# Global attention in a hybrid encoder: the high and low parts of the probabilities side by side, as one moving operand of 512 columns

## The chip, the cores and the metric

The kernel runs on 1 core of one Trainium2 chip. The metric is the device time of one execution in microseconds (us). The kernel before takes 2157.99 us, the median of 3 runs (2155.97 to 2158.89).

## What is computed

One encoder layer is applied to a prompt of 1024 tokens and a sample of 256 tokens, each with 16 learned meta tokens in front of it, at a model width of 2048. A projection gives queries, keys, values and gates of two groups of 8 heads, of 128 numbers each. Group A attends globally, with 2 key and value heads shared by 4 query heads each; group B attends in a window around each token of a 64-wide grid, plus the meta tokens. The results are gated and go through an output projection. The change is in group A alone:

```python
def global_gqa(q, k, v):
    scale = HEAD_DIM ** -0.5
    def attend(qb):                      # a block of queries
        qg = qb.reshape(B, L, N_KV_A, G, HEAD_DIM)
        s = jnp.einsum('blkgd,bskd->bkgls', qg, k).astype(jnp.float32) * scale
        p = jax.nn.softmax(s, axis=-1).astype(v.dtype)
        o = jnp.einsum('bkgls,bskd->blkgd', p, v)
        return o.reshape(B, L, D_A)
    ...
ya = global_gqa(qa, ka, va) * jax.nn.silu(za)
```

Everything is float32.

## The kernel before

**Products in three parts.** TensorE (PE) takes most operands in a reduced form of float32 (`F32R`). To keep the precision, `split` (L65 to L67) makes two pieces of an operand: ScalarE (ACT) copies it into the reduced form, the high part, and VectorE (DVE) subtracts that from the full value, which leaves the low part. A product then takes three matmuls that add up in one PSUM tile: high by high, low by high, and high by low.

**Stages.** `chunk1` projects the sample's 256 tokens, 240 of the prompt's and the meta tokens, and attends for the sample. `chunk2` projects the prompt's other 784 tokens, attends globally for the whole prompt (head by head, each in 4 blocks of 256 queries), and then does the windowed heads. `outproj` is the output projection. In the profile shown here `chunk2`'s global blocks lie between about 700 and 1335 us.

**A global block** is one call of `attend`. For each pair of key tiles (128 keys each) three matmuls a tile (L377 to L379) put scores into `sp`; ACT copies them into a tile `S` (L381) and DVE keeps a running maximum (L385, L387). GpSimd (POOL) takes the maximum over partitions (`all_max`, L328); DVE subtracts it (L397), ACT takes the exponential (L398), and DVE and POOL make the sum (L401 to L407, L346). Then come the values: for each pair of key tiles `split` makes `ph` and `pl`, 512 columns each, from `S`, and for each key tile three matmuls of 256 columns add into `po`, with the transposed output of 128 rows by 256 queries:

```python
nc.tensor.matmul(po[:], vh, ph[:, i, :], start=j == 0, stop=False)    # L418
nc.tensor.matmul(po[:], vl, ph[:, i, :], start=False, stop=False)     # L419
nc.tensor.matmul(po[:], vh, pl[:, i, :], start=False, stop=False)     # L420
```

`vh` and `vl` are the two parts of the value tile, the stationary operand, which PE loads anew for each matmul. One matmul for the meta tokens ends the sum (L421). `put_y` turns the sum of probabilities into its reciprocal (L353 to L356), multiplies `po` by the gate (L362, DVE, or L359 in a windowed block), then by the reciprocal (L363), and stores the result (L364, on SyncE's queue SP).

The prompt has 8 heads with 4 blocks of 8 key tiles each, 256 key tiles in all. The sample has 8 heads with one block of 2 key tiles each, 16 in all.

**What sets the order.** Nothing here is ordered by hand: a scheduler with its own estimate of durations puts the instructions of each engine into one fixed order when the program is built. Every engine then works through its own list in that order. So between the matmuls of a block stand matmuls of the next head's projection (`pp`, L227 to L229), which fill the time in which a block waits for ACT, DVE and POOL. Buffers are limited: `po` has one buffer in PSUM (pool `op`), `ph` and `pl` have two each, `sp` two.

Of the kernel before, what the change touches and what calls it, by code (L numbers as in the profile page):

```python
# [12 lines left out]
F32 = mybir.dt.float32  # L13
F32R = mybir.dt.float32r
BF16 = mybir.dt.bfloat16
AF = mybir.ActivationFunctionType
ALU = mybir.AluOpType
# [4 lines left out]
P = 128  # L22
# [13 lines left out]
ALIGN = 128  # L36
# [4 lines left out]
QB = 256  # L41
# [18 lines left out]
class Kern:  # L60
# [288 lines left out]
    def put_y(self, po, tot, zs, ydst):  # L349

        nc = self.nc
        r = self.t.tile([P, QB], F32, tag="t", name="r")
        nc.scalar.activation(r[:], tot[:], AF.Ln)  # L353
        nc.scalar.activation(r[:], r[:], AF.Exp, scale=-1.0)
        nc.vector.tensor_tensor(out=tot[:], in0=tot[:], in1=r[:], op=ALU.mult)
        nc.vector.scalar_tensor_tensor(out=r[:], in0=tot[:], scalar=2.0, in1=r[:], op0=ALU.subtract, op1=ALU.mult)  # L356
        y = self.y.tile([P, QB], F32, tag="y", name="y")
        if len(zs.shape) == 3:
            nc.vector.tensor_tensor(out=y[:].rearrange("p (g r) -> p g r", g=4), in0=po[:].rearrange("p (g r) -> p g r", g=4),  # L359
                                    in1=zs, op=ALU.mult)  # L360
        else:
            nc.vector.tensor_tensor(out=y[:], in0=po[:], in1=zs, op=ALU.mult)  # L362
        nc.vector.scalar_tensor_tensor(out=y[:], in0=y[:], scalar=-1.0, in1=r[:], op0=ALU.mult, op1=ALU.mult)  # L363
        self.ystore = nc.sync.dma_start(ydst, y[:].rearrange("p (g r) -> p g r", g=ydst.shape[1])).ins  # L364

    def attend(self, q, zs, keys, meta, vals, vmeta, ydst):

        nc = self.nc
        nt = len(keys)
        qh, ql = q[:, 0, :], q[:, 1, :]  # L370
        S = []
        mx = None
        for p in range(nt // 2):
            ps = self.sp.tile([P, 2, QB], F32, tag="sp", name="sp")
            for i in range(2):
                kh, kl = keys[2 * p + i]
                nc.tensor.matmul(ps[:, i, :], kh, qh, start=True, stop=False)  # L377
                nc.tensor.matmul(ps[:, i, :], kh, ql, start=False, stop=False)  # L378
                nc.tensor.matmul(ps[:, i, :], kl, qh, start=False, stop=True)  # L379
            s = self.s.tile([P, 2, QB], F32, tag="S", name="S")  # L380
            nc.scalar.copy(s[:], ps[:])  # L381
            S.append(s)
            if p == 1:
                mx = self.mx.tile([P, 2, QB], F32, tag="mx", name="mx")
                nc.vector.tensor_tensor(out=mx[:], in0=S[0][:], in1=ps[:], op=ALU.max)  # L385
            elif p > 1:
                nc.vector.tensor_tensor(out=mx[:], in0=mx[:], in1=ps[:], op=ALU.max)  # L387
        pm = self.sp.tile([P, 2, QB], F32, tag="sp", name="sm_ps")
        sm = self.meta_scores(pm[:, 0, :], meta, qh, ql, 1.0)
        src = S[0] if mx is None else mx  # L390
        m1 = self.t.tile([P, QB], F32, tag="t", name="m1")
        nc.vector.tensor_tensor(out=m1[:], in0=src[:, 0, :], in1=src[:, 1, :], op=ALU.max)
        ma = self.all_max(m1, sm)
        mb = ma[:].unsqueeze(1).to_broadcast([P, 2, QB])
        for p in range(nt // 2):
            s = S[p][:]
            nc.vector.tensor_tensor(out=s, in0=s, in1=mb, op=ALU.subtract)  # L397
            nc.scalar.activation(s, s, AF.Exp, scale=SCALE)  # L398
            if p == 1:
                acc = self.mx.tile([P, 2, QB], F32, tag="mx", name="acc")  # L400
                nc.vector.tensor_tensor(out=acc[:], in0=S[0][:], in1=S[1][:], op=ALU.add)  # L401
            elif p > 1:
                nc.vector.tensor_tensor(out=acc[:], in0=acc[:], in1=s, op=ALU.add)
        pm3 = self.meta_probs(sm, ma, SCALE)
        src = S[0] if nt == 2 else acc
        a1 = self.t.tile([P, QB], F32, tag="t", name="a1")
        nc.vector.tensor_tensor(out=a1[:], in0=src[:, 0, :], in1=src[:, 1, :], op=ALU.add)  # L407
        tot = self.all_sum(a1, sm)
        yield
        po = self.op.tile([P, QB], F32, tag="po", name="po")  # L410
        for j in range(nt):
            p, i = divmod(j, 2)
            if i == 0:
                ph = self.ph.tile([P, 2, QB], F32R, tag="ph", name="ph", align_bytes=ALIGN)
                pl = self.ph.tile([P, 2, QB], F32R, tag="pl", name="pl", align_bytes=ALIGN)
                self.split(ph[:], pl[:], S[p][:])
            vh, vl = vals[j]
            nc.tensor.matmul(po[:], vh, ph[:, i, :], start=j == 0, stop=False)  # L418
            nc.tensor.matmul(po[:], vl, ph[:, i, :], start=False, stop=False)  # L419
            nc.tensor.matmul(po[:], vh, pl[:, i, :], start=False, stop=False)  # L420
        nc.tensor.matmul(po[:], vmeta, pm3[:], start=False, stop=True)  # L421
        self.put_y(po, tot, zs, ydst)

    def attend_sample(self, q, zs, k, km, vals, vmeta, tab, ydst):

        nc = self.nc
        ps = self.sp.tile([P, 2, QB], F32, tag="sp", name="sp")
        ps = ps[:].rearrange("p a b -> p (a b)")
        for i in range(2):
            nc.tensor.matmul(ps[:, HALF * i:HALF * i + HALF], k[:, P * i:P * i + P], q[:, 64 * i:64 * i + HALF], start=True, stop=True)  # L430
        pm = self.sp.tile([P, 2, QB], F32, tag="sp", name="sm_ps")
        hl = self.ph.tile([P, 2, QB], F32R, tag="ph", name="qhl", align_bytes=ALIGN)
        self.split(hl[:, 0, :], hl[:, 1, :], q)
        sm = self.meta_scores(pm[:, 0, :], km, hl[:, 0, :], hl[:, 1, :], SCALE)
        s = self.s.tile([P, 2, QB], F32, tag="S", name="S")
        s = s[:].rearrange("p a b -> p (a b)")
        w = 2 * HALF
        self.lasts = nc.vector.scalar_tensor_tensor(out=s[:, :w], in0=ps[:, :w], scalar=SCALE, in1=tab, op0=ALU.mult, op1=ALU.add).ins

        def ap(t, off, dims):  # L440
            return bass.AP(t.tensor, t.offset + off, [list(t.ap[0])] + dims)

        def gather(name, op):

            m = self.t.tile([P, QB], F32, tag="t", name=name)
            nc.vector.tensor_copy(ap(m[:], 0, [[192, 2], [1, 64]]), ap(s, 0, [[320, 2], [1, 64]]))
            nc.vector.tensor_tensor(out=m[:, 64:192], in0=s[:, 64:192], in1=s[:, 192:320], op=op)
            return m

        ma = self.all_max(gather("m1", ALU.max), sm)  # L450
        v = ap(s, 0, [[HALF, 2], [1, HALF]])
        nc.vector.tensor_tensor(out=v, in0=v, in1=ap(ma[:], 0, [[64, 2], [1, HALF]]), op=ALU.subtract)
        nc.scalar.activation(s[:, :w], s[:, :w], AF.Exp)
        pm3 = self.meta_probs(sm, ma, 1.0)
        tot = self.all_sum(gather("a1", ALU.add), sm)
        yield
        po = self.op.tile([P, QB], F32, tag="po", name="po")
        nc.tensor.matmul(po[:], vmeta, pm3[:], start=True, stop=False)
        for i in range(2):
            nc.tensor.matmul(po[:, 64 * i:64 * i + HALF], vals[:, i, :], s[:, HALF * i:HALF * i + HALF], start=False, stop=i == 1)  # L460
        self.put_y(po, tot, zs, ydst)

    def attend_strip(self, q, qf, zs, k, meta, vals, vmeta, tab, w, ydst):
# [3 lines left out]
        nc = self.nc  # L467
# [25 lines left out]
        def ap(t, off, dims):  # L493
            return bass.AP(t.tensor, t.offset + off, [list(t.ap[0])] + dims)
# [13 lines left out]
        v = ap(sb, 0, [[192, 2], [1, 192]])  # L508
        nc.vector.tensor_tensor(out=v, in0=v, in1=ap(ma[:], 0, [[64, 2], [1, 192]]), op=ALU.subtract)
        nc.scalar.activation(sb[:, :384], sb[:, :384], AF.Exp)  # L510
        pm3 = self.meta_probs(sm, ma, 1.0)
        tot = self.mx.tile([P, 2, QB], F32, tag="mx", name="tot")[:, 0, :]
        self.all_sum(gather("a1", ALU.add), sm, tot)
        yield
        po = self.op.tile([P, QB], F32, tag="po", name="po")
        nc.tensor.matmul(po[:], vmeta, pm3[:], start=True, stop=False)
        for t in (0, 3, 1, 2):
            a, e = groups[t]
            nc.tensor.matmul(po[:, 64 * a:64 * e], vals[:, t, :], part(sa, sb, t), start=False, stop=t == 2)  # L519
# [826 lines left out]
```

## Time and profile before

| What | us |
|---|---|
| Time, median of 3 runs | 2157.99 |
| Time of the profiled execution | 2156.31 |
| Its span, first to last instruction | 2154.5 |
| PE busy, 11745 matmuls | 2147.4 |
| PE loading weights (beside matmuls) | 1878.4 |
| DVE busy | 1666.1 |
| ACT busy | 1190.9 |
| POOL busy | 524.0 |

The span is the profiled execution's time but for 1.8 us. "Busy" adds up what an engine's instructions cover. The ends of matmuls are modelled, and consecutive matmuls overlap in the profile: one of 256 columns is shown as 0.28 us long while the next one starts 0.12 us after it. So a matmul's price is the distance between the starts of two in a row, not its length. PE's granted clock is 1.00 over the whole span. A wait is the idle time of an engine before an instruction; it is put down to the work that ended last before it.

### The profile page before, as it was taken

The page shows a single profiled execution, that of the slowest core. Times are in us where ns is not written, and L with a number is a line of the kernel's source. Part 1 is how long each engine was busy: PE and PEld are TensorE (multiplying, and loading weights), DVE is VectorE, ACT ScalarE, POOL GpSimd, SP SyncE. Part 2 cuts the span into 40 slices and gives each one's busy share as a digit, 9 for nine tenths or more (in the row PEclk, how much of TensorE's full clock was granted, in tenths as well). Part 3 has the DMA queues.
Part 4 walks back from the last instruction along what each step waited for, and adds up shares of the span by engine and source line. Part 5 has one row for each costly group of instructions (what it writes and reads, how often), then busy time and mean ns, then how long its engine had stood idle before and what let it go on. Part 6 is the DMA issues. An engine that isn't in the chain of part 4 may idle for free.

```text
span 2154.5 us, 34001 instructions
## 1 busy us (share of the span) xinstructions
PE 2147.4 (100%) x11745; PEld 1878.4 (87%) x11745; DVE 1666.1 (77%) x3013; ACT 1190.9 (55%) x2419; POOL 524.0 (24%) x250
## 2 busy tenths in 40 slices
PE   9999999999999999999999999999999999999999
PEld 7888888888888999998999999989999888888887
DVE  7698977788874899996799988777787786545763
ACT  7677644454665777776677775444444454232230
POOL 1142422222221223231133224333333311000000
PEclk9999999999999999999999999999999999999999
DMA  8666789988654333334233244554433364762663
GB/s 294 215 193 220 238 291 320 341 280 281 212 191 133 97 102 106 110 97 142 91 110 100 95 129 150 184 161 135 138 124 123 114 215 140 242 234 91 234 225 107
DMA packets 257420, 377.24 MB, mean 175 GB/s; under 512 B 43072, under 2 KB 108768, under 8 KB 257248
## 3 DMA queue, kind: packets, MB, share of 16 engines
q1 hardware_dynamic: 257248, 375.07, 53.7%
q8 instruction: 92, 1.51, 0.3%
q14 instruction: 80, 0.66, 0.1%
HBM read 281.01 MB, written 100.38 MB: 177 GB/s over the span
## 4 chain that ended last, share of the span: by engine, by line
PE 98%; DVE 1%; DMA 1%; SPq 0%; issue 0%; ACT 0%; DVEq 0%
PE pp L229 22%; PE pp L227 22%; PE pp L228 22%; PE pq L1072 6%; PE pq L1070 6%; PE pq L1071 6%; PE po L519 2%; PE sp L485 2%; PE sp L378 1%; PE sp L379 1%; PE po L420 1%; PE sp L377 1%; PE po L419 1%; PE po L418 1%; PE tp L540 0%; PE sm_ps L316 0%
## 5 line engine op out<-in xcount | busy, mean ns | idle before, releaser
L227 PE MATMUL pp<-x,wh 128*128 128x512 f32 (+1 forms) x1664 | 654.0, 394 | 0.6 <-ACT wh L66 0.3
L229 PE MATMUL pp<-x,wl 128*128 128x512 f32 (+1 forms) x1664 | 647.8, 390 | 0.2 <-DVE wl L67 0.2
L228 PE MATMUL pp<-x,wh 128*128 128x512 f32 (+1 forms) x1664 | 647.9, 390 | 0.0
L229 PEld LDWEIGHTS pp<-x,wl 128*128 128x128 f32 x1664 | 312.5, 188 | 61.4 <-DVE wl L67 0.8
L227 PEld LDWEIGHTS pp<-x,wh 128*128 128x128 f32 x1664 | 312.4, 188 | 55.6 <-ACT wh L66 2.0
L228 PEld LDWEIGHTS pp<-x,wh 128*128 128x128 f32 x1664 | 312.9, 188 | 51.9
L262 POOL PARTITION_ALL_REDUCE m<-ms x78 | 223.1, 2860 | 352.5 <-ACT ms L260 300.3
L67 DVE TENSOR_TENSOR wl<-wr,wh 128x512 fp32r<-128x512 f32 (+2 forms) x287 | 209.6, 732 | 107.2 <-ACT wh L66 80.4
L346 POOL PARTITION_ALL_REDUCE tot<-a x80 | 181.0, 2262 | 433.5 <-DVE a L343 419.8
L66 ACT CAST wh<-wr 128x512 fp32r<-128x512 f32 (+2 forms) x287 | 173.5, 611 | 162.5 <-PE pp L228 147.8
L228 PE MATMUL pp<-xb,wh 128*128 128x272 f32 x832 | 240.8, 289 | 0.0
L227 PE MATMUL pp<-xb,wh 128*128 128x272 f32 x832 | 239.6, 288 | 0.0
L229 PE MATMUL pp<-xb,wl 128*128 128x272 f32 x832 | 239.0, 287 | 0.0
L328 POOL PARTITION_ALL_REDUCE ma<-m x80 | 113.3, 1417 | 447.8 <-DVE m L326 436.3
L1072 PE MATMUL pq<-wm,yl 128*128 128x512 f32 x560 | 218.3, 390 | 0.6 <-DVE yl L67 0.6
L1070 PE MATMUL pq<-wm,yh 128*128 128x512 f32 x560 | 218.3, 390 | 0.0
L1071 PE MATMUL pq<-wm,yh 128*128 128x512 f32 x560 | 218.0, 389 | 0.0
L227 PEld LDWEIGHTS pp<-xb,wh 128*128 128x128 f32 x832 | 156.5, 188 | 7.5
L228 PEld LDWEIGHTS pp<-xb,wh 128*128 128x128 f32 x832 | 156.5, 188 | 7.4
L229 PEld LDWEIGHTS pp<-xb,wl 128*128 128x128 f32 x832 | 157.4, 189 | 0.1
L1072 PEld LDWEIGHTS pq<-wm,yl 128*128 128x128 f32 x560 | 105.1, 188 | 22.9 <-DVE yl L67 1.0
L1071 PEld LDWEIGHTS pq<-wm,yh 128*128 128x128 f32 x560 | 105.1, 188 | 21.6
(218 smaller groups left out, 3951.9 us busy)
## 6 DMA issues: line engine op xcount, KB each, us to landing
wr<-in_w_in SPq DMA_DIRECT2D x413, 256.0 KB, 3.5
wld<-wl SPq DMA_DIRECT2D x132, 256.0 KB, 4.3
wl<-wld SPq DMA_DIRECT2D x132, 256.0 KB, 3.1
yr<-yd SPq DMA_DIRECT2D x35, 512.0 KB, 5.2
wq<-in_w_out SPq DMA_DIRECT2D x64, 256.0 KB, 5.1
td<-wq SPq DMA_DIRECT2D x64, 256.0 KB, 4.4
ww<-td SPq DMA_DIRECT2D x64, 256.0 KB, 5.2
ww<-in_w_out SPq DMA_DIRECT2D x48, 256.0 KB, 5.1
```

What stands on the lines that cost most here:

```text
L66: self.hi = nc.scalar.copy(hi, full).ins
L67: return nc.vector.tensor_tensor(out=lo, in0=full, in1=hi.bitcast(F32), op=ALU.subtract).ins
L227: nc.tensor.matmul(p[:, :n], wh[:, k, :], xh[:, :n], start=first, stop=False)
L228: nc.tensor.matmul(p[:, :n], wh[:, k, :], xl[:, :n], start=False, stop=False)
L229: self.lastmm = nc.tensor.matmul(p[:, :n], wl[:, k, :], xh[:, :n], start=False, stop=last).ins
L262: nc.gpsimd.partition_all_reduce(m2[:], ms[:], P, RED.add)
L328: nc.gpsimd.partition_all_reduce(ma[:], m1[:], P, RED.max)
L346: nc.gpsimd.partition_all_reduce(tot[:], a1[:], P, RED.add)
L485: nc.tensor.matmul(dst, k[:, o:o + P], qfv[:, a:e, :], start=True, stop=True)
L1070: nc.tensor.matmul(ps, yh, wh, start=k == 0, stop=False)
L1071: nc.tensor.matmul(ps, yh, wl, start=False, stop=False)
L1072: self.lastmm = nc.tensor.matmul(ps, yl, wh, start=False, stop=k == 7).ins
```

## The change

The low part no longer has a tile of its own. `split` writes the high and the low part of each key tile side by side into one tile `hl`, and one matmul takes both, 512 columns, with `vh`. Its product goes into a `po` of two halves: what comes from the high part into half 0, what comes from the low part into half 1. The product of `vl` and the high part, and that of the meta tokens, go into half 0. `put_y` adds the halves: ACT copies half 1 into `y`, DVE adds half 0 to it, and then come the gate and the reciprocal as before. The tile `po` fills 512 columns of PSUM in place of 256, for the windowed blocks and the sample's too, which use half 0 of it alone.

```diff
@@ put_y
         else:
-            nc.vector.tensor_tensor(out=y[:], in0=po[:], in1=zs, op=ALU.mult)
+            v = po
+            if len(po.shape) == 3:
+                nc.scalar.copy(y[:], po[:, 1, :])
+                v = y[:]
+                nc.vector.tensor_tensor(out=v, in0=po[:, 0, :], in1=v, op=ALU.add)
+            nc.vector.tensor_tensor(out=y[:], in0=v, in1=zs, op=ALU.mult)
@@ attend
-        po = self.op.tile([P, QB], F32, tag="po", name="po")
+        po = self.op.tile([P, 2, QB], F32, tag="po", name="po")
         for j in range(nt):
             p, i = divmod(j, 2)
             if i == 0:
-                ph = self.ph.tile([P, 2, QB], F32R, tag="ph", name="ph", align_bytes=ALIGN)
-                pl = self.ph.tile([P, 2, QB], F32R, tag="pl", name="pl", align_bytes=ALIGN)
-                self.split(ph[:], pl[:], S[p][:])
+                hl = self.ph.tile([P, 2, 2, QB], F32R, tag="ph", name="ph", align_bytes=ALIGN)
+                self.split(hl[:, :, 0, :], hl[:, :, 1, :], S[p][:])
             vh, vl = vals[j]
-            nc.tensor.matmul(po[:], vh, ph[:, i, :], start=j == 0, stop=False)
-            nc.tensor.matmul(po[:], vl, ph[:, i, :], start=False, stop=False)
-            nc.tensor.matmul(po[:], vh, pl[:, i, :], start=False, stop=False)
-        nc.tensor.matmul(po[:], vmeta, pm3[:], start=False, stop=True)
+            nc.tensor.matmul(po[:], vh, hl[:, i], start=j == 0, stop=False)
+            nc.tensor.matmul(po[:, 0, :], vl, hl[:, i, 0, :], start=False, stop=False)
+        nc.tensor.matmul(po[:, 0, :], vmeta, pm3[:], start=False, stop=True)
@@ attend_sample, attend_strip
-        po = self.op.tile([P, QB], F32, tag="po", name="po")
-        nc.tensor.matmul(po[:], vmeta, pm3[:], start=True, stop=False)
+        po = self.op.tile([P, 2, QB], F32, tag="po", name="po")[:, 0, :]
+        nc.tensor.matmul(po, vmeta, pm3[:], start=True, stop=False)
```

The scheduler makes its order anew. From soon after the start of `chunk2`'s windowed blocks PE's order is the same as before; in the global blocks of the prompt, and around the blocks of the sample's global heads, it is another. In the changed kernel the matmuls of the values are L422 (512 columns) and L423 (256 columns), that of the meta tokens is L424, ACT's copy is L364, DVE's addition L366, and the products with gate and reciprocal L367 and L368.

On PE, at the first value matmuls of the first global block of the prompt, before (`va` is the value tile, `pp` a projection's sum, `x` and `xb` its input, `wh` and `wl` the two parts of its weights):

```order
L418 MATMUL po<-ph,va 128x256
L419 MATMUL po<-ph,va 128x256
L227 MATMUL pp<-xb,wh 128x272
L228 MATMUL pp<-xb,wh 128x272
L229 MATMUL pp<-xb,wl 128x272
L227 MATMUL pp<-xb,wh 128x272
L228 MATMUL pp<-xb,wh 128x272
L420 MATMUL po<-pl,va 128x256
L418 MATMUL po<-ph,va 128x256
```

The same place now:

```order
L227 MATMUL pp<-x,wh 128x512
L422 MATMUL po<-ph,va 128x512
L423 MATMUL po<-ph,va 128x256
L422 MATMUL po<-ph,va 128x512
L423 MATMUL po<-ph,va 128x256
L228 MATMUL pp<-x,wh 128x512
L229 MATMUL pp<-x,wl 128x512
L422 MATMUL po<-ph,va 128x512
```

Before, two matmuls with the high part stand ahead of five projection matmuls, and the first one with the low part behind these. Now the value matmuls of a pair of key tiles stand together, behind the projection matmuls.

On DVE, at the end of the same block, before (`z` is the gate, `za` a later gate in the making, `m`, `Sm` and `S` belong to the next block):

```order
L355 TENSOR_TENSOR tot<-tot,r 128x256
L326 TENSOR_TENSOR m_7682<-m_7682,Sm 16x256
L362 TENSOR_TENSOR y<-po,z 128x256
L356 SCALAR_TENSOR_TENSOR r<-tot,r 128x256
L363 SCALAR_TENSOR_TENSOR y<-y,r 128x256
```

And now:

```order
L326 TENSOR_TENSOR m_7664<-m_7664,Sm 16x256
L366 TENSOR_TENSOR y<-po,y 128x256
L302 TENSOR_TENSOR z<-pp,rb_320 128x272
L307 SCALAR_TENSOR_TENSOR za<-z,za 128x512
L367 TENSOR_TENSOR y<-y,z 128x256
L368 SCALAR_TENSOR_TENSOR y<-y,r 128x256
```

The addition stands where the product with the gate stood, and that product has moved behind work for the projection.

On ACT, at the same place now (before, there was no instruction of the block between these):

```order
L305 ACTIVATE za<-za 128x512
L364 COPY y<-po 128x256
L306 ACTIVATE za<-za 128x512
L211 CAST wh<-wr 128x512
L304 ACTIVATE za<-z 128x272
```

The copy of half 1 stands among activations for a gate and ahead of the split of a weight tile.

More of the change, by code (lines that the diff above doesn't have):

```diff
@@ L358, in put_y @@
         if len(zs.shape) == 3:
-            nc.vector.tensor_tensor(out=y[:].rearrange("p (g r) -> p g r", g=4), in0=po[:].rearrange("p (g r) -> p g r", g=4),
+            nc.vector.tensor_tensor(out=y[:].rearrange("p (g r) -> p g r", g=4), in0=po.rearrange("p (g r) -> p g r", g=4),
                                     in1=zs, op=ALU.mult)
         else:
-            nc.vector.tensor_tensor(out=y[:], in0=po[:], in1=zs, op=ALU.mult)
+            v = po
[4 more added lines that the diff above has]
+            nc.vector.tensor_tensor(out=y[:], in0=v, in1=zs, op=ALU.mult)
         nc.vector.scalar_tensor_tensor(out=y[:], in0=y[:], scalar=-1.0, in1=r[:], op0=ALU.mult, op1=ALU.mult)
@@ L514, in attend_strip @@
         yield
-        po = self.op.tile([P, QB], F32, tag="po", name="po")
-        nc.tensor.matmul(po[:], vmeta, pm3[:], start=True, stop=False)
+        po = self.op.tile([P, 2, QB], F32, tag="po", name="po")[:, 0, :]
+        nc.tensor.matmul(po, vmeta, pm3[:], start=True, stop=False)
         for t in (0, 3, 1, 2):
```

## Prediction

> **What bounds the kernel now.** I read the page first: the engines, the slices of the span, and the chain that ended last.
>
> ```profile
> PE 2147.4 (100%) x11745; PEld 1878.4 (87%) x11745; DVE 1666.1 (77%) x3013; ACT 1190.9 (55%) x2419; POOL 524.0 (24%) x250
> PEclk9999999999999999999999999999999999999999
> PE 98%; DVE 1%; DMA 1%; SPq 0%; issue 0%; ACT 0%; DVEq 0%
> ```
>
> PE is covered from end to end, at its full granted clock, and the chain that decides the end is PE in 98% of its length. Next come the stretches of the span, by stage. The columns are length, then busy us of PE, of its weight loads, of DVE, ACT and POOL with their counts.
>
> ```profile
> 0.00:700.00 700.00, 697.28 (x3341) 588.95 (x3342) 548.95 (x926) 417.30 (x824) 180.41 (x75) 1.00 0.76 247
> 700.00:1335.00 635.00, 635.00 (x4117) 581.90 (x4116) 561.88 (x1024) 458.55 (x932) 187.73 (x91) 1.00 0.35 108
> 1100.00:1200.00 100.00, 100.00 (x653) 91.78 (x652) 93.23 (x170) 72.10 (x149) 34.14 (x17) 1.00 0.33 103
> 1850.00:2050.00 200.00, 200.00 (x884) 165.62 (x883) 120.61 (x178) 60.04 (x110) 0.00 (x0) 1.00 0.56 198
> ```
>
> The second row holds the prompt's global blocks, where nearly all of the change lies: PE has no idle time in 635 us. DVE is busy 561.88 us there, 88%, and 93% in the densest 100 us: the engine that would become the bound next. Last I read PE's waits, all of them:
>
> ```profile
> PE warm L641 <- DVE wz L638: 1.2, 1, 1.2
> PE tp L296 <- DVE vt L289: 0.7, 1, 0.7
> PE pq L1072 <- DVE yl L67: 0.6, 1, 0.6
> PE pp L227 <- ACT wh L66: 0.3, 1, 0.3
> PE pp L227 <- ACT x L114: 0.3, 1, 0.3
> PE pp L229 <- DVE wl L67: 0.2, 1, 0.2
> ```
>
> They are 3.3 us in all, and none is for a global block. So a microsecond taken from PE's list shortens the kernel by one, and a change elsewhere shortens nothing. What counts is how much less time PE needs for a key tile, and whether a wait arises.
>
> **The change part by part: the matmuls.** The by-line view of L418 gives the count of key tiles and the timeline of PE the distance between starts (first column start, second length, in us).
>
> ```profile
> L418 PE MATMUL po<-ph,va x256: 276/280/286, 704.5 to 1333.2; 128*128 128x256 f32 x128
> L418 PE MATMUL po<-ph,vs x16: 276/280/365, 106.5 to 281.3; 128*128 128x256 f32 x16
> 706.68 0.39 PE L227 MATMUL pp<-x,wh 128*128 128x512 f32 x1
> 706.91 0.40 PE L228 MATMUL pp<-x,wh 128*128 128x512 f32 x1
> ...
> 708.07 0.39 PE L227 MATMUL pp<-x,wh 128*128 128x512 f32 x1
> ...
> 710.76 0.28 PE L420 MATMUL po<-pl,va 128*128 128x256 f32 x1
> ...
> 711.95 0.28 PE L421 MATMUL po<-Pm,vm 128*128 128x256 f32 x1
> 712.07 0.28 PE L228 MATMUL pp<-xb,wh 128*128 128x272 f32 x1
> ...
> 712.81 0.28 PE L228 MATMUL pp<-xb,wh 128*128 128x272 f32 x1
> ```
>
> From 706.68 to 708.07 six matmuls of 512 columns start: 1.39 / 6 = 0.2317 us each. From 710.76 to 711.95 ten of 256 columns: 1.19 / 10 = 0.119 us. So 256 more columns cost 0.1127 us, 0.44 ns a column, and what a matmul costs beyond its columns is 0.119 - 0.1127 = 0.0063 us. The row of 272 columns tests this: six in 0.74 us, 0.1233 us, against 0.119 + 16 x 0.00044 = 0.126. Columns set the pace, not the number of matmuls.
>
> The change takes away no column: a key tile has 3 x 256 = 768 before and 512 + 256 = 768 now. It takes away one matmul and one weight load: 0.357 us before, 0.2317 + 0.119 = 0.3507 now, 0.0063 us less. There are 256 + 16 = 272 key tiles, so PE's list is 272 x 0.0063 = 1.7 us shorter. Bounds: in 1850 to 2050 us there are matmuls of 512 columns alone, 884 in 200 us, 0.2262 us each; with that a tile saves 0.0118 us, 3.2 us in all. The other bound is a fixed part of nothing, so 0. I take 1.7, since its rows stand beside the value matmuls, in the same stage and with the same neighbours.
>
> The Trainium skill ("TensorE: Matmul & The Clock Gate", section "Back-to-back issue gap") gives the distance of two warm matmuls as N / 2.4 + 2.5 ns; by its 2.5 ns for each matmul the estimate would be 272 x 2.5 ns = 0.7 us. The rows here show 6.3 ns and a slower pace in the columns too (0.2317 us where the formula has 0.216), so the rows are taken.
>
> **The split.** L66 and L67 now write every other 256 columns of a piece, in the same number of instructions and elements. For a pattern in pieces the nearest rows are the product with the gate, once with a gate in four pieces (L359) and once in one (L362):
>
> ```profile
> L362 DVE TENSOR_TENSOR y<-po,z x32: 404/413/426, 712.5 to 1335.2; 128x256 f32<-128x256 f32 x32
> L359 DVE TENSOR_TENSOR y<-po,z x32: 405/413/425, 1351.2 to 1807.1; 128x256 f32<-128x256 f32 x32
> L67 DVE TENSOR_TENSOR pl<-S,ph 128x512 fp32r<-128x512 f32 x128 | 94.0, 745 | 7.3 <-ACT ph L66 4.6 <-PE po L420 2.5
> ```
>
> Both take 413 ns, so I take nothing. The upper bound is two pieces at the price of two instructions of 256 columns, 2 x 413 = 826 ns against 745: 0.08 us on each of 128, 10 us of DVE's time in 635, where DVE has 73 idle. So it is hidden on either bound.
>
> **The first matmul now waits for the low part.** Before, L418 and L419 needed the high part alone; now L422 needs both. What that costs is seen where the trace had the least room, at the second pair of rows here (ACT's L66 makes the high part, DVE's L67 the low one):
>
> ```profile
> 749.93 0.41 DVE L362 TENSOR_TENSOR y<-po,z 128x256 f32<-128x256 f32 x1
> 753.20 0.61 ACT L66 CAST ph<-S 128x512 fp32r<-128x512 f32 x1
> 755.90 0.67 DVE L67 TENSOR_TENSOR pl<-S,ph 128x512 fp32r<-128x512 f32 x1
> 756.10 0.28 PE L418 MATMUL po<-ph,va 128*128 128x256 f32 x1
> 759.37 0.28 PE L420 MATMUL po<-pl,va 128*128 128x256 f32 x1
> ```
>
> The low part is done at 755.90 + 0.67 = 756.57, and L418 starts at 756.10: in the old order it would come 0.47 us too early. But L420, which needed that part before, starts 2.8 us behind it. The order lists for the first global block show that the scheduler has moved the first value matmul behind the projection matmuls, to where L420 stood. So I take no wait, with 0.47 us for a place where it failed. Behind a waiting L422 on PE stand the projection and the next scores, that is everything.
>
> **The sum of the halves.** A block gets a copy of 128 x 256 out of PSUM on ACT and an addition on DVE, 40 of each. The addition is like L362, 0.413 us. For the copy the nearest rows are a smaller and a larger read of PSUM by ACT:
>
> ```profile
> L319 ACT ACTIVATE Sl<-sm_ps x48: 381/382/386, 91.8 to 1314.9; 48x256 f32<-48x256 f32 x48
> L381 ACT COPY S<-sp x136: 559/586/591, 91.2 to 1310.8; 128x512 f32<-128x512 f32 x136
> ```
>
> It lies between 0.382 and 0.586 us; I take 0.38, since both reads have 256 columns. In the 32 prompt blocks that is 12 us for ACT, which has 635.00 - 458.55 = 176 us idle, and 13 us for DVE, which has 73. Neither reaches the path. The copy waits for PE's last value matmul, and behind it on ACT stand an activation of a gate and the split of a weight tile (L306, L211 in the order list), which PE needs later. The work that hides this is the projection, put ahead of time in weight buffers.
>
> The single `po` becomes free later by these two instructions, 0.38 + 0.41 = 0.8 us. In the rows above `po` is read until 750.34 and first written by the next block at 756.10, 5.8 us later. That cover stays.
>
> **The sum.** 1.7 us off PE, nothing added: the profiled execution's 2156.31 us would be 2154.6, and the median of the runs, 2157.99, which lies 1.7 us above that execution, 2156.3. I forecast 2156.3 us. A measurement of this kernel can tell about 0.2%, 4.3 us, from no change, so this counts as the same.
>
> **The rivals.** First, slower: the low part comes too late. Place: the first L422 of a pair. For it speaks that four engines work through lists made from estimates, and that DVE is 93% busy in the densest stretch. Against it: the order lists, and the 2.8 us that L420 had. If each of the 40 blocks waited 0.47 us once, it would be 18.8 - 1.7 = 17.1 us slower, 2175.1 us. It decides from (4.3 + 1.7) / 0.47 = 13 waits on.
>
> Second, slower: DVE becomes the bound. In the densest 100 us lie 5 blocks, so the additions bring 93.2 to 95.3 us. The 4.7 left, over 20 splits in 100 us, are used up if a split takes 0.23 us more than its 0.745. At one and a half times, 0.37 us more, DVE would lack 20 x 0.37 - 4.7 = 2.7 us in 100, 17 us in 635: 2174 us. Against it stands the pair of rows at 413 ns.
>
> Third, faster by far: each weight load costs PE time of its own. For it speaks that loads cover 581.90 of 635 us. A load is shown 0.19 us long and matmuls of 256 columns start 0.119 us apart:
>
> ```profile
> 710.77 0.19 PEld L418 LDWEIGHTS po<-ph,va 128*128 128x128 f32 x1
> ```
>
> If the difference, 0.07 us, were paid for each load, 272 fewer would give 19 us, 2139 us. Against it: the loads overlap each other and the matmuls, and the pace fits the columns to 0.0063 us. The same section of the Trainium skill has a sustained pace of about 81 ns for N = 128 and 131 ns for N = 512; by these, worked out as a straight line, a matmul would have some 64 ns of its own, an estimate of 17 us. The trace disagrees: 0.2317 us for 512 columns.
>
> Fourth, faster: the new order removes waits elsewhere. All waits of PE are 3.3 us, so with 1.7 it gives 5.0 at most, 2153.0 us.
>
> **How the numbers follow.** Forecast 0.84, of which 0.03 lies beyond 0.2% (its upper bound of 3.2 us and the spread of the runs). First rival 0.06. Second rival 0.04, a quarter of it small enough to count as the same. Third 0.02, fourth 0.04. Faster: 0.03 + 0.02 + 0.04 = 0.09. Slower: 0.06 + 0.03 = 0.09. Same: 0.82. The range: the saving's bounds put the median between 2157.99 - 3.2 = 2154.8 and 2158.0. The runs of before lie from 2.0 below to 0.9 above their median, which makes 2152.8 and 2158.9; three waits of 0.47 us more at the upper end make it 2160.3.
>
> **What would show it.** Right: value matmuls of 512 columns start some 0.23 us before the next, those of 256 some 0.12; in the global blocks PE has no wait; ACT's copy takes about 0.38 us, the split 0.75; `po`'s next writer still comes microseconds after its reader. The global stretch would then be 256 x 0.0063 = 1.6 us shorter, all else the same. Wrong: PE waits on L422 for DVE's L67 (first rival), DVE covered without a gap (second), or a tile that saves tens of nanoseconds (third).

## The result: 3.2 us less, where 1.7 were forecast

| | before | changed |
|---|---|---|
| Median of 22 runs each, us | 2157.02 (2155.94 to 2160.07) | 2153.86 (2153.14 to 2155.57) |
| Profiled execution, us | 2156.31 | 2154.02 |
| Its span, us | 2154.5 | 2152.2 |
| All waits of PE, us | 3.3 | 2.0 |

The ratio is 0.9986 with a 95% interval of 0.998 to 0.9992: the changed kernel is 3.2 us faster, between 1.7 and 4.3. This lies inside the forecast's range and inside the 0.2% that was called the same. It is nearly twice the 1.7 us of the sum, which is the lower end of the interval. Of the 2.4 us between the forecast of 2156.3 and the 2153.86 measured, 1.0 comes from the starting point: the median of 22 runs of before lies that much below that of the first three.

The page of the changed kernel has the same shape as before: PE from end to end.

```profile
PE 2146.3 (100%) x11473; PEld 1866.0 (87%) x11473; DVE 1675.4 (78%) x3053; ACT 1204.0 (56%) x2459; POOL 530.0 (25%) x250
PE 99%; DMA 0%; DVE 0%; SPq 0%; issue 0%; ACT 0%
```

PE has 272 matmuls and 272 loads less, DVE and ACT have 40 instructions more each. The columns are as many as before, and PE's busy time fell by 1.1 us only. The same stretches by stage:

```profile
700.00:1335.00 635.00, 635.00 (x3867) 571.12 (x3866) 566.82 (x1049) 467.57 (x961) 192.53 (x90) 1.00 0.36 109
1100.00:1200.00 100.00, 100.00 (x611) 89.89 (x610) 94.29 (x172) 73.57 (x152) 38.74 (x16) 1.00 0.34 101
```

PE still has no idle time in the global blocks. DVE went from 561.88 to 566.82 us, and from 93.23 to 94.29 in the densest 100 us: closer to the bound, not at it. These are all waits of PE:

```profile
PE warm L644 <- DVE wz L641: 1.2, 1, 1.2
PE pp L227 <- ACT wh L66: 0.8, 3, 0.3
```

None is for `po` or for a low part. The waits for `vt` and `yl` that stood in before (0.7 and 0.6 us) are gone, though the change touches neither. The changed instructions, by tile:

```profile
L422 PE MATMUL po<-ph,va x256: 387/394/403, 704.8 to 1341.8; 128*128 128x512 f32 x128
L423 PE MATMUL po<-ph,va x256: 274/281/286, 705.1 to 1342.0; 128*128 128x256 f32 x128
L364 ACT COPY y<-po x40: 359/372/377, 109.5 to 1342.5; 128x256 f32<-128x256 f32 x40
L366 DVE TENSOR_TENSOR y<-po,y x40: 403/411/425, 110.4 to 1343.3; 128x256 f32<-128x256 f32 x40
```

The copy takes 0.372 us (0.38 was assumed), the addition 0.411 (0.413). The split, by line, in the global stretch:

```profile
L67 DVE TENSOR_TENSOR ph<-S,ph 128x512 fp32r<-128x512 f32 x126 | 94.4, 757 | 13.3 <-ACT ph L66 13.1
```

This is a mean of 757 ns where it was 745. The mean is moved by a few long ones. All splits of `S`, before and now, with the shortest, the median and the longest:

```profile
L67 DVE TENSOR_TENSOR pl<-S,ph x136: 668/678/1578, 102.7 to 1329.3; 128x512 fp32r<-128x512 f32 x136
L67 DVE TENSOR_TENSOR ph<-S,ph x136: 669/677/2724, 102.6 to 1337.2; 128x512 fp32r<-128x512 f32 x136
```

The median is 678 ns before and 677 now: writing in pieces costs nothing. And PE's timeline at the first pairs of the first global block:

```profile
704.83 0.40 PE L422 MATMUL po<-ph,va 128*128 128x512 f32 x1
705.06 0.28 PE L423 MATMUL po<-ph,va 128*128 128x256 f32 x1
705.18 0.39 PE L422 MATMUL po<-ph,va 128*128 128x512 f32 x1
705.41 0.28 PE L423 MATMUL po<-ph,va 128*128 128x256 f32 x1
705.53 0.40 PE L228 MATMUL pp<-x,wh 128*128 128x512 f32 x1
...
706.70 0.40 PE L227 MATMUL pp<-x,wh 128*128 128x512 f32 x1
```

A matmul of 512 columns starts 0.23 us before the next, one of 256 columns 0.12. From 704.83 to 705.53 two tiles pass in 0.70 us, 0.35 each, which is what the sum had. From the starts of all matmuls, a key tile takes 351.1 ns now and took 353.9 before: 2.8 ns less, 0.8 us for 272 tiles.

Where the 2.3 us between the two spans arise can be read at matmuls behind which the same work lies in both kernels. First before:

```profile
276.25 0.28 PE L296 MATMUL tp<-ident,vt 128*16 128x128 f32 x1 [0.72 <-DVE vt L289]
708.07 0.39 PE L227 MATMUL pp<-x,wh 128*128 128x512 f32 x1
1381.47 0.39 PE L229 MATMUL pp<-x,wl 128*128 128x512 f32 x1
```

And the same matmuls now:

```profile
275.03 0.27 PE L296 MATMUL tp<-ident,vt 128*16 128x128 f32 x1
707.40 0.39 PE L227 MATMUL pp<-x,wh 128*128 128x512 f32 x1
1379.50 0.53 PE L229 MATMUL pp<-x,wl 128*128 128x512 f32 x1
```

At `tp` before waits 0.72 us for `vt`, and the changed kernel, in its new order, does not: its lead grows there by 0.8 us. From 0.67 us at 707.40 the lead grows to 1.97 at 1379.50. So 1.3 us arise in the prompt's global blocks, in which 252 of the 272 tiles lie, and the other 0.2 us elsewhere.

So two explanations stood against each other. Theory A: the fused matmul itself saves the time, by what it spares PE for each matmul. Theory B, the rival: the order that the scheduler made anew saves it, and the fused matmul little. A third thing was worth a run of its own, the rival of the prediction by which a weight load costs PE time.

### The profile page after: what moved, and what is told of

Its sections match the earlier page's. It is cut to its first block, busy times and chain, and to the rows that moved or that the text cites. A ratio compares the mean times of both kernels' runs of the same rounds, so it can differ in the third digit from the quotient of the medians.

```text
span 2152.2 us, 33487 instructions
## 1 busy us (share of the span) xinstructions
PE 2146.3 (100%) x11473; PEld 1866.0 (87%) x11473; DVE 1675.4 (78%) x3053; ACT 1204.0 (56%) x2459; POOL 530.0 (25%) x250
## 4 chain that ended last, share of the span: by engine, by line
PE 99%; DMA 0%; DVE 0%; SPq 0%; issue 0%; ACT 0%
PE pp L227 22%; PE pp L229 22%; PE pp L228 22%; PE pq L1075 6%; PE pq L1074 6%; PE pq L1073 6%; PE po L422 3%; PE po L522 2%; PE sp L488 2%; PE sp L383 2%; PE sp L384 2%; PE sp L382 1%; PE po L423 1%; PE tp L543 0%; PE sm_ps L316 0%; PE sm_ps L315 0%
## 5 line engine op out<-in xcount | busy, mean ns | idle before, releaser
L262 POOL PARTITION_ALL_REDUCE m<-ms x78 | 237.8, 3049 | 324.5 <-ACT ms L260 251.2
L346 POOL PARTITION_ALL_REDUCE tot<-a x80 | 175.8, 2198 | 476.2 <-DVE a L343 449.2
```

Source lines behind the costliest of these rows:

```text
L262: nc.gpsimd.partition_all_reduce(m2[:], ms[:], P, RED.add)
L346: nc.gpsimd.partition_all_reduce(tot[:], a1[:], P, RED.add)
```

## The experiments

All ratios are to the kernel before on the same chip. The changed kernel ran again in the same rounds as two_of_256, layout_alone and no_halves_sum; the times of the others are set against its first measurement. The first eight leave the scheduler free to make its order anew, and the next three pin it.

**after_again: the changed kernel once more.** No edit.

> The changed kernel once more, on the same chip and in the same rounds as the three kernels beside it, as their reference. Both theories expect the known ratio to the kernel before, 0.9986 (0.998 to 0.9992), some 3 us less. In its trace a key tile should cost PE as in the first profile: 0.233 us for the matmul of 512 columns and 0.118 us for the one of 256.

Measured: 2153.61 us (2153.25 to 2155.07), ratio 0.9985 (0.9976 to 0.9994). The gain repeats. The profiled execution's span is 2153.3 us, 1.1 longer than in the first profile of the same program. PE's waits:

```profile
PE warm L644 <- DVE wz L641: 1.2, 1, 1.2
PE pp L227 <- ACT wh L66: 0.5, 2, 0.3
PE tp L296 <- DVE vm L67: 0.5, 1, 0.5
PE tp L296 <- DVE vt L289: 0.2, 1, 0.2
```

The waits of `tp` are here and were not in the other execution of this program. Worked out from the starts of all matmuls, the value matmuls agree in the two executions to 0.0 us in sum. Single waits come and go; the pace does not. Against before, the lead grows here by the same 0.8 us at the `tp` of 276 us and by 1.1 us in the global blocks.

**two_of_256: the layout, the halves and their sum stay, but the fused matmul is two of 256 columns.**

```diff
-            nc.tensor.matmul(po[:], vh, hl[:, i], start=j == 0, stop=False)
+            nc.tensor.matmul(po[:, 0, :], vh, hl[:, i, 0, :], start=j == 0, stop=False)
             nc.tensor.matmul(po[:, 0, :], vl, hl[:, i, 0, :], start=False, stop=False)
+            nc.tensor.matmul(po[:, 1, :], vh, hl[:, i, 1, :], start=False, stop=False)
```

> The changed kernel with its matmul of 512 columns issued as two of 256, into the same two halves; tile layout, waits and the sum of the halves stay. Theory A (the saving is what a matmul costs beyond its columns): the key tile is back at 3 matmuls, so the time is 0.7 us (by 2.7 ns a tile, as the two traces give it) to 1.7 us (by 6.3 ns, as forecast) above the changed kernel. Theory B (the saving comes from another order of the instructions, which removed waits of PE outside the value matmuls): the time follows its own waits of PE and not the count of matmuls; if it stays at the changed kernel's time with the same few waits, B holds alone.

Measured: 2166.14 us, ratio 1.0044 (1.0031 to 1.0056), 12.5 us above after_again on the same chip. PE's longest waits, but for `warm`:

```profile
PE sp L382 <- DVE mx L392: 3.4, 3, 1.5
PE po L422 <- ACT ph L66: 1.3, 1, 1.3
PE pq L1076 <- DVE yl L67: 1.0, 1, 1.0
```

But for the second, these sit at places that have nothing to do with the edit: the order is another one, with new waits. The run can't tell what the fused matmul is worth.

**layout_alone: before with the two parts in one piece; three matmuls of 256 columns, one `po` of 256, no sum of halves.**

```diff
-                ph = self.ph.tile([P, 2, QB], F32R, tag="ph", name="ph", align_bytes=ALIGN)
-                pl = self.ph.tile([P, 2, QB], F32R, tag="pl", name="pl", align_bytes=ALIGN)
-                self.split(ph[:], pl[:], S[p][:])
+                hl = self.ph.tile([P, 2, 2, QB], F32R, tag="ph", name="ph", align_bytes=ALIGN)
+                self.split(hl[:, :, 0, :], hl[:, :, 1, :], S[p][:])
... (the three matmuls read hl[:, i, 0, :] and hl[:, i, 1, :])
```

> The kernel before with the high and low parts side by side in one tile, but with its three matmuls of 256 columns, one output of 256 columns and no sum of halves. PE has the same list as before, in an order that the scheduler makes anew. Theory A: the time of the kernel before, 2157 us, within 0.5 us. Theory B: a new order alone can move the time by 1 to 2 us, in step with PE's waits in the trace, so it may come near the changed kernel's 2154 us.

Measured: 2162.8 us, ratio 1.0026 (1.0016 to 1.0037), 5.8 us slower than before, with the same work on every engine. Theory A had 2157 us within 0.5 for it, theory B a move of 1 to 2 us; it moved by more, and the other way. PE's longest waits, but for `warm`:

```profile
PE sm_ps L315 <- DVE mx L387: 3.3, 2, 2.1
PE pq L1071 <- DVE yl L67: 0.9, 1, 0.9
```

**no_halves_sum: the changed kernel without the copy and the addition.** Half 1 is computed and left out of the output.

```diff
-                nc.scalar.copy(y[:], po[:, 1, :])
-                v = y[:]
-                nc.vector.tensor_tensor(out=v, in0=po[:, 0, :], in1=v, op=ALU.add)
+                v = po[:, 0, :]
```

> The changed kernel without the sum of the halves: ACT's copy and DVE's addition are left out, so half 1, the product of the low part, is not in the output. Theory (both): these 80 instructions are covered, so the time is that of the changed kernel within 1 us. Rival: they delay something that PE waits for, and it is faster by more than 1 us.

Measured: 2155.99 us, ratio 0.9995 (0.9986 to 1.0004), 2.4 us above after_again with 80 instructions less. Less work took longer, so the remade order decides this run too, and moves the time by nearly as much as the change is worth. It can't tell what the sum of the halves costs.

**three_by_8 and two_by_8: every value matmul eight times over,** before's three and the changed kernel's two (whose edit is shown). The output has the values' part eight times.

```diff
-            nc.tensor.matmul(po[:], vh, hl[:, i], start=j == 0, stop=False)
-            nc.tensor.matmul(po[:, 0, :], vl, hl[:, i, 0, :], start=False, stop=False)
+            for n in range(8):
+                nc.tensor.matmul(po[:], vh, hl[:, i], start=j == 0 and n == 0, stop=False)
+                nc.tensor.matmul(po[:, 0, :], vl, hl[:, i, 0, :], start=False, stop=False)
```

> The kernel before with the three value matmuls of each key tile issued eight times over, so that the output has the values eight times. It measures the price of a key tile: 7 x 272 = 1904 tiles more. Theory A as forecast: 0.357 us a tile, 680 us more than the kernel before. By the first two traces: 0.354 us, 674 us more.

> The changed kernel with the two value matmuls of each key tile issued eight times over (values eight times in the output): 1904 tiles more. Theory A as forecast: 0.3507 us a tile, 668 us more than the changed kernel, 12 us less growth than with three matmuls. By the first two traces 0.351 us, 5 us less growth. Theory B alone: no difference in growth. Rival (each weight load costs PE time of its own, 0.07 us): 130 us less growth.

Measured: 2824.74 us, ratio 1.3088 (1.3069 to 1.3108), and 2825.94 us, ratio 1.3096 (1.3076 to 1.3115). Seven more sets for 272 tiles are 1904 tiles: (2824.74 - 2157.78) / 1904 = 0.3503 us a tile with three matmuls, and (2825.94 - 2153.86) / 1904 = 0.3530 with two. From the starts of all matmuls in the traces it is 0.3523 and 0.3520. So in long runs of value matmuls a matmul saved is worth 0.3 ns by the trace, and nothing by the times, where the forecast's 6.3 ns would give 12 us. If each load cost 0.07 us of PE's time, the second would have grown by 1904 x 0.07 = 133 us less. That rival falls.

**no_low_part: before without the product of the low part.** The low part is still made; L420's product is left out.

```diff
-            nc.tensor.matmul(po[:], vh, pl[:, i, :], start=False, stop=False)
```

> The kernel before without the product of the values and the low part (L420 left out; the low part is still made): 512 columns a tile in place of 768. If columns are what PE pays for, 272 x 0.118 = 32 us less than the kernel before, 2125 us. If the number of matmuls and weight loads were what counts, the change, which takes away as many matmuls, would have given nearly the same, and it gave 3 us.

Measured: 2140.1 us, ratio 0.9918 (0.9901 to 0.9934), 17.7 us less than before where 32 were expected. The value matmuls did get 30.8 us shorter, from 106.1 to 75.3 us by the starts of all of them. Of the 13.1 us between the two, 8.3 are waits of PE, 11.6 us here and 3.3 before; the view doesn't show the rest. The longest but for `warm` are:

```profile
PE po L418 <- ACT ph L66: 3.3, 2, 1.7
PE tp L296 <- DVE vt L289: 1.1, 2, 0.9
PE sp L484 <- DVE S L489: 0.9, 1, 0.9
```

So 31 us off PE's list did not shorten this kernel by 31. The order was made anew here too, and how much of the difference is the order's own wasn't separated.

**halves_sum_x6: copy and addition six times in a chain.** Each pair repeats the first one's work.

```diff
-                nc.scalar.copy(y[:], po[:, 1, :])
                 v = y[:]
-                nc.vector.tensor_tensor(out=v, in0=po[:, 0, :], in1=v, op=ALU.add)
+                for _ in range(6):
+                    nc.scalar.copy(v, po[:, 1, :])
+                    nc.vector.tensor_tensor(out=v, in0=po[:, 0, :], in1=v, op=ALU.add)
```

> The changed kernel with the copy and the addition of the halves done six times in a chain (half 1 is added more than once): 200 more instructions on each of ACT and DVE, some 75 us and 82 us, and the single output tile in PSUM is held 4 us longer. DVE had 68 us idle in the 635 us of the global blocks and gets 66 us more there, ACT 60 of 167. Theory: DVE is then full, PE waits here and there, and the time grows by 2 to 20 us. If it grows by less than 2 us, the cover is larger than the busy times say; by over 20 us, the held output tile is what PE waits for.

Measured: 2238.36 us, ratio 1.0375 (1.0359 to 1.039), some 85 us above the changed kernel, where 2 to 20 were expected. PE's longest waits:

```profile
PE sp L383 <- DVE mx L391: 21.3, 4, 8.4
PE po L423 <- DVE ph L67: 15.7, 5, 9.2
PE po L423 <- DVE y L367: 8.3, 6, 2.8
```

The held tile `po` (third row) is the smallest of these. By the code each copy waits for DVE and each addition for ACT, and what is queued behind them on DVE comes late: the maximum of the next block and the low part. All waits of PE are some 57 us. A lower granted clock falls together with them, 0.90 and 0.91 in three stretches of 100 us between 800 and 1300 us where before has 1.00, and what each is worth of the 85 us wasn't separated. One such exchange is hidden, a chain of six is not.

**The pinned orders.** The free runs had shown that the scheduler's order moves the time by more than the change. So these three build one kernel, read off the order of every engine, and build the other with that order fixed:

```python
for e, key in order:              # the engine's instructions, in the other kernel's order
    i = by[key]
    if e in last:
        tc.add_manual_dep(i, last[e].name, ...)   # order of issue alone, no semaphore
    last[e] = i
```

**two_after_order** has the changed kernel's order and all its work, with two matmuls of 256 columns at the place of each fused one. **before_work_after_order** is before's work in the changed kernel's order: three matmuls and one `po` of 256, no sum of halves, the product with the gate at the place of the addition. **after_work_before_order** is the changed kernel's work in before's order: fused matmul and that of `vl` where before had the low part's matmul; the place of ACT's copy, which before doesn't have, is left to the scheduler.

> The changed kernel with its matmul of 512 columns as two of 256, one behind the other, pinned to the order of the changed kernel: nothing but the number of matmuls and weight loads differs. As forecast (6.3 ns a tile): 1.7 us above the changed kernel, 2155.4 us. By the tiles that were issued eight times (0.3 ns a tile): the same time within 0.3 us. By the first two traces (2.7 ns): 0.7 us more. Without the pinned order it took 12.5 us more; if it does again, the order was not the cause of that.

> The kernel before (three matmuls of 256 columns a key tile, high and low part in tiles of their own, no sum of halves), with every engine's instructions pinned to the order of the changed kernel: where that has its matmul of 512 columns stands the one with the high part, and the one with the low part stands right behind the one with the low part of the values. Theory B (the order is what made it faster): the time of the changed kernel and at most 0.7 us more, 2153.7 to 2154.4 us. Theory A (one matmul less for each key tile): the time of the kernel before, 2157.0 us.

> The changed kernel with every engine pinned to the order of the kernel before: the matmul of 512 columns and the one with the low part of the values stand where the matmul with the low part stood, the addition of the halves and the product with the gate where that product stood; ACT's 40 copies are free in their place. Theory B: 0 to 0.7 us below the kernel before, 2156.3 to 2157.0 us. Theory A: the time of the changed kernel, 2153.7 us.

| | us | ratio |
|---|---|---|
| two_after_order | 2156.85 | 0.9999 (0.999 to 1.0008) |
| before_work_after_order | 2155.99 | 0.9995 (0.9986 to 1.0004) |
| after_work_before_order | 2175.37 | 1.0087 (1.0073 to 1.01) |

In the new order without the fused matmul the time is that of before, twice. two_after_order lies 3.0 us above the changed kernel, more than any of its three prices gave; 1.5 us of that are two single waits, 1.0 for `vt` and the one near 1245 us named below. An order that alone gave the changed kernel's 0.9986 lies outside the first interval and at the edge of the second; a share of up to some 2 us by the first, 3 by the second, that the order gave isn't excluded by the times. The first value matmuls by tile, in two_after_order:

```profile
L444 PE MATMUL po<-ph,va x256: 274/280/288, 705.9 to 1345.0; 128*128 128x256 f32 x128
```

And in before_work_after_order:

```profile
L444 PE MATMUL po<-ph,va x256: 275/280/290, 704.8 to 1343.6; 128*128 128x256 f32 x128
```

From the first to the last tile it takes 1345.0 - 705.9 = 639.1 and 1343.6 - 704.8 = 638.8 us; the changed kernel, in the same order, takes 1341.8 - 704.8 = 637.0. That is 1.8 to 2.1 us more for 256 tiles. In both runs PE's matmuls other than those of the values stand in the changed kernel's order, one for one, and from start to start before_work_after_order falls back evenly in these blocks, with no single step over 0.12 us. PE's timeline of two_after_order at the pairs shown above:

```profile
705.90 0.28 PE L444 MATMUL po<-ph,va 128*128 128x256 f32 x1
706.02 0.28 PE L446 MATMUL po<-ph,va 128*128 128x256 f32 x1
706.13 0.28 PE L447 MATMUL po<-ph,va 128*128 128x256 f32 x1
...
707.80 0.40 PE L234 MATMUL pp<-x,wh 128*128 128x512 f32 x1
```

Four tiles and two projection matmuls take 1.90 us here, 706.70 - 704.83 = 1.87 in the changed kernel. Over all 272 tiles, matmul against matmul, the two of 256 columns take 118.7 + 118.1 = 236.8 ns, the fused one 232.7: 4.1 ns, 1.1 us in all, 1.3 with the neighbours among the value matmuls. Of the 2.1 us, 0.5 is one wait near 1245 us (fourth row below). The 0.3 to 0.5 us that are left in each of the two runs lie between the matmuls around, and why isn't shown. All waits of PE over 0.2 us in two_after_order:

```profile
PE warm L671 <- DVE wz L668: 1.2, 1, 1.2
PE tp L303 <- DVE vt L296: 1.0, 1, 1.0
PE pp L234 <- ACT x L121: 0.4, 1, 0.4
PE sp L393 <- DMA q<-qd: 0.3, 1, 0.3
PE pq L1102 <- DVE yl L74: 0.3, 1, 0.3
```

The third pinned kernel is 21.5 us slower than the changed one with its work. Its longest waits of PE, but for `warm`:

```profile
PE tp L303 <- DVE vt L296: 2.1, 1, 2.1
PE sp L393 <- DVE mx L401: 2.1, 2, 1.1
PE po L442 <- DVE ph L74: 2.0, 3, 0.9
PE sm_ps L322 <- DVE mx L403: 1.6, 3, 1.2
```

Neither theory had this: they gave 2153.7 and 2156.3 to 2157.0 us. The third row is the first rival of the prediction, a fused matmul that waits for the low part: it comes three times in 40 blocks. The others are DVE in arrears. In before's order the addition stands where the gate's product stood, and there it waits 11.8 us for the copy, with all that is queued behind it; in the changed kernel that wait is 8.1 us. How much of the 21.5 us follows from it isn't shown:

```profile
DVE y L373 <- ACT y L371: 11.8, 8, 2.9
```

**before_again: one look at the kernel before,** to see what changes from one execution to the next.

> A second profile of the kernel before, to see which of PE's waits come back in every execution: those behind the vt and yl tiles, 0.7 and 0.6 us, should be there again, and the span should be 2154 to 2156 us.

Measured: 2156.19 us, span 2154.4. Its waits but for `warm`:

```profile
PE tp L296 <- DVE vt L289: 0.7, 1, 0.7
PE pq L1072 <- DVE yl L67: 0.7, 1, 0.7
PE pp L227 <- ACT wh L66: 0.6, 2, 0.3
```

The first is as it was, the second 0.1 us longer, the third twice as long. So the wait for `vt`, near 276 us, stands in both executions of before.

## Why the prediction was right, and where its size was off

- **Columns set the pace.** Held. 272 matmuls and loads less took 1.1 us off PE's busy time, and a load doesn't cost the 0.07 us of the third rival (three_by_8, two_by_8).
- **The price of a matmul beyond its columns, 6.3 ns, 1.7 us in all.** This term was mis-sized. From before to the changed kernel a tile got 2.8 ns cheaper, 0.8 us in all. In the same order it is 4.1 ns for the two matmuls that became one and 4.7 to 5.0 for the whole tile, 1.1 to 1.4 us, since the three matmuls are a little slower in the new order (355.8 and 356.1 ns a tile, 353.9 in before's). In an eightfold run it is 0.3 ns. The step set 0.2317 us, a distance of projection matmuls, against 0.119 us, one short run of value matmuls. But the fused matmul has 0.2327, and the 256-column ones have 0.1179 on the mean over the prompt's blocks of before. Its own test had shown how fine the rows were: the 272 columns came out 2.7 ns below what the price gave, nearly half of the term. The Trainium skill's 2.5 ns for a matmul ("TensorE: Matmul & The Clock Gate", section "Back-to-back issue gap") lies between the 0.3 and the 4.1 ns of these runs, and so was nearer than the value taken.
- **The split, hidden.** Held, and nothing was there to hide: the median is 677 ns, and was 678.
- **No wait for the low part.** Held, and only with the new order: in before's order this wait appears, 2.0 us in 3 blocks. The price was set at 0.47 us a place and is 0.7 there on the mean. The first rival left out the addition that waits for the copy in an engine that works in order; DVE's 11.8 us of that stand beside it, though what they cost in time isn't separated.
- **Copy and addition, hidden.** Held: 0.372 and 0.411 us, and PE waits for neither (no_halves_sum, with its order made anew, doesn't test this). Of `po`'s cover, 5.8 us at the pair shown before, 4.7 us are left at the smallest, by the rows of its readers and writers in the global blocks. The cover has an end, as halves_sum_x6 shows.
- **The fourth rival, waits that the new order removes.** It came true in part, beside the forecast. The wait for `vt` near 276 us, 0.7 us, stands in both executions of before and in neither of the changed kernel, which gains 0.8 us there, nor at this place in the two runs pinned to its order; the matmuls around it stand in another order now. The forecast counted this wait among the 3.3 us and gave its removal a chance of 0.04.

Of the 3.2 us (1.7 to 4.3) the traces place 1.1 to 1.3 in the prompt's global blocks, 0.7 of them in the value matmuls' own distances, and 0.8 at the wait for `vt`. The remaining 1.1 us or so were not settled: they may lie in small waits that come and go, since one profiled execution of a kernel isn't its median. So the mechanism was right, and its price too high (6.3 ns, where 2.8 were measured against before). That the whole came out above the forecast rests on what the sum didn't have: this wait, the distances of the matmuls around, and the part not settled. The saving's own bounds, 0 to 3.2 us, reached down to 2154.8 us. The measured 2153.86 lies below that, by the 1.0 us of the starting point, and is inside the range because this allowed for the spread of the runs too. That it came in so is in part luck.

## What to carry to other kernels

Where an engine is covered from end to end, count what it is paid by, here columns: a matmul saved at equal columns was worth 0.3 to 4 ns. Where a scheduler makes the order anew, an edit of such a size can't be read from two free builds: the same work came out between 2153.9 and 2175.4 us in two orders, so pin the order before a gain or a loss is put down to the edit. A hand-over between two engines that work in order can cost what is queued behind it: one copy and one addition a block were hidden, six in a chain cost some 85 us.

## What was not expected of the hardware

Between two executions of one program all value matmuls kept their distances, 0.0 us apart in sum, while waits for a DVE result came and went by up to 0.5 us each, and the spans differed by 1.1. A fused matmul of 512 columns took 232.7 ns where the projection's of the same width took 226 to 232. And in halves_sum_x6, where PE stood idle in places, the mean granted clock was 0.985, against 1.00 in before and in the changed kernel. The mean length of the splits was moved by some 15 of 128 that took 0.9 to 2.7 us, and what held those up isn't shown.
